# Hybrid GDN/GLA encoder step on one core: two weights' conversions moved ahead of the first copies, sample's transposes widened to 128 rows, the last chunk stored earlier

## The chip, the cores and the metric

The kernel runs on one core of a Trainium2 chip. Its engines are TensorE (PE, matrix products and transposes), VectorE (DVE), ScalarE (ACT), GpSimd (POOL) and SyncE (SP); each works through its own list of instructions in order, and they meet through semaphores. DMA transfers are issued from the lists of SP, POOL and, here and there, ACT. The metric is the device time of one launch in microseconds, smaller is better; of the kernel before there are three timed runs and one profiled execution.

## The reference

One step of a one-layer encoder trunk, for 512 prompt tokens and, with states and caches of their own, 64 sample tokens, at model width 1024, all in float32:

```python
x = x + mixer(rmsnorm(x))        # gated DeltaNet and gated linear attention, merged by gates
x = x + cross_attn(rmsnorm(x))   # 4 heads into 256 memory tokens
x = x + conv_ffn(rmsnorm(x))     # up-projection, depthwise conv, silu gate, down-projection
y = rmsnorm(x) * norm_final
```

In the gated DeltaNet part, tokens go in chunks, and each chunk needs a triangular solve:

```python
kb = kc * bc[..., None]
a_kk = jnp.where(strict, jnp.einsum('nbhcd,nbhsd->nbhcs', kb, kc) * decay, 0.0)
wu = lax.linalg.triangular_solve(eye + a_kk, rhs, left_side=True, lower=True, unit_diagonal=True)
```

The cross attention is `softmax(q k^T / 16) v` per head. The outputs are `y` for prompt and sample, the new states and convolution rows, and the memory's keys and values.

## The kernel before

Features lie on the 128 partitions and the T = 576 tokens (512 prompt, then 64 sample) along the free axis. For a product, a 1024-wide weight comes as tiles of 128 x 1024. To keep float32's accuracy, weight and activation are each split into a high part (`h`, rounded to the format that PE multiplies fast) and a low part (`lo`), and PE forms three products: h by h, h by lo, lo by h (`mm3`).

A weight gets its two parts in `emit_weight` (L621) and `split_summed` (L653): SP loads the raw tile; ACT writes its rounded negative into `lo` (an ACTIVATE with scale −1, "w<-wr") and its rounded copy into `h` (a CAST); then POOL's queue issues a DMA that adds the raw weight from memory to `lo` ("w<-wt", the accumulate), which leaves the rounding error there. A product with that weight's `lo` thus waits for ACT, POOL's queue and the transfer in turn. There are 6 tiles for weight parts (`WB`) and 4 for raw weights (`RAWB = 4`, L29); `weight()` (L717) gives back the parts of weights that are used up, and `fetch` starts later ones.

Nearly all instructions go through a planner, the class `Driver` (L251). It keeps an estimate of when each engine and operand is free, and places an instruction in its engine's list by its planned start; generators of work (`yield`) are run side by side, and products of the large matrices are put between the steps of small chains. So the order on an engine can change where the code that makes a chain changes.

*Start*, in `main` (L1711): the first three weights are split by hand (`wpart`). Then PE multiplies them with all of x, 3 x 8 blocks. `conv_raw` (L1766) makes ACT and DVE copy the three results to `u`; it calls for the results' last product. Only behind it stand `fetch(3)`, which emits the fourth weight and later ones, and the last four calls of `sq_act`. The fourth weight feeds the products ("za") that follow. The small power of the first norm is taken on POOL (`rt`); from it come `dg`, which PE needs to spread the norm over partitions (`rbc`), and `ba`, the input of the gates.

*Sample's triangular solve*, in `c_gdn` (L1135), whose call for sample has n = 64 rows: `xi` holds the inverse as it grows, four heads beside each other. For each of the five `LEVELS`, its odd block columns are copied to `xo`, PE transposes them (L1263), a product with the odd columns of N (`no`, made by `odd_keys`, L1243) follows (L1271), and ACT and DVE mask the result and write it back. `xo` and `no` are tiles of their own; the operands of PE span 64 partitions.

*Sample's attention*, in `c_att` (L1546): `e` holds the exponentials of a group of tokens; the group of the sample has 64 rows. Once per head, two blocks of it are transposed into `pS` (L1591) and copied to `pst`.

*Tail*, from L2344: `half` forms the down-projection's last products, `half_evac` adds them to x, squares and scales; `sums` lets PE add up the squares for a chunk of tokens; `roots` takes the power on DVE and POOL (`rt`); `flip` transposes a chunk (8 transposes) to token-major; `put_out` scales it on ACT and DVE and issues two stores, from SP's list but for one store each of chunks 0 and 1, which ACT issues. Chunks 0 to 3 are prompt's, of 128 tokens; chunk 4 is the sample's 64. In the order of the code: `half(1)` on the first 256 tokens, its evacuation, chunk 3, the sums of chunks 0 and 1, chunk 4, then chunks 0 and 1.

Memory for work tiles is a pool of 57 slots (`NS`) of 584 columns (`SLOT`).

Of the kernel before, what the change touches and what calls it, by code (L numbers as in the profile page):

```python
# [25 lines left out]
SLOT = 584  # L26
HT = T // 2
NS = 57
# [484 lines left out]
def tile_trunk(ctx, tc, xT, memT, wt, wd, vec, cst, w0, wgate, st_gdn, st_conv, st_gla, st_ffn, ckT, cv,  # L513
# [345 lines left out]
    def sum_tile(w=T):  # L859
        acc = slot("acc")  # L860
        G.memset(acc[:, w:w + 8], 0.0)
        return acc
# [10 lines left out]
    def c_rstat(key, accs, n, sample, delay, out=None, at=TP):  # L873
# [8 lines left out]
        if sample:  # L882
            k += 1
            ssq(accs, n, 72, ps)
            G.memset(rin, 1.0)
            V.tensor_scalar(rin[0:64, n:n + 1], ps[0:64, n:n + 1], 1.0 / D, EPS, op0=ALU.mult, op1=ALU.add)
# [196 lines left out]
    def head_norms(*tiles):  # L1083
# [12 lines left out]
        for (o3, n, k), ss in zip(tiles, sums):  # L1096
            on3 = r4(slot("on")[0:n, 0:128 * k])
            V.tensor_tensor(on3, o3, ss[0:n, 0:k].unsqueeze(2).broadcast_to([n, k, 128]), op=ALU.mult)
            ons.append(on3)
# [9 lines left out]
    def head_norm(o3, n, k, box, rq=None):  # L1109
# [13 lines left out]
        on = slot("on")  # L1123
        on3 = r4(on[0:n, 0:128 * k])
# [10 lines left out]
    def c_gdn(h):  # L1135
# [93 lines left out]
        xi = slot("xi")  # L1229
        for i in range(4):  # L1230
            V.scalar_tensor_tensor(xi[0:n, n * i:n * i + n], pk[0:n, n * i:n * i + n], rr[0:n, 4 * SX + i:4 * SX + i + 1],
                                   negm1[0:n, 0:n], op0=ALU.mult, op1=ALU.mult)
# [10 lines left out]
        def odd_keys(li):  # L1243
            no = small(f"no{me}", 2, 256)
            A.copy(no[0:n, 0:w].rearrange("p (a b) -> p a b", b=LEVELS[li]), odd(N_.rearrange("p a b -> p (a b)"), LEVELS[li]))
            return no

        no = odd_keys(0)
        xo = small(f"xo{me}", 1, 256)
# [10 lines left out]
        for li, b in enumerate(LEVELS):  # L1260
            pt = sm()
            for c in range(w // 128):
                PE.transpose(pt[:, n * c:n * c + n], xo[0:n, 128 * c:128 * c + 128], ident[0:n, 0:n])  # L1263
# [6 lines left out]
            for c in range(w // 128):  # L1270
                PE.matmul(p1[:, 128 * c:128 * c + 128], no[0:n, 128 * c:128 * c + 128], even(xi[0:n, 256 * c:256 * c + 256], b), start=True, stop=True)  # L1271
# [3 lines left out]
            if b < LEVELS[-1]:  # L1275
                no = odd_keys(li + 1)
                xo = small(f"xo{me}", 1, 256)
# [22 lines left out]
        if n == 128:  # L1300
            pt2 = sm()
            tt = slot("T2")
            G.memset(tt[0:64, 0:256], 0.0)
            for i in range(4):
                PE.matmul(pt2[64:128, 64 * i:64 * i + 64], N_[:, i, 64:128], xi3[:, i, 0:64], start=True, stop=True)
            V.tensor_copy(tt[64:128, 0:256], pt2[64:128, 0:256])
# [41 lines left out]
        for i in range(4 if h < 4 else 0):  # L1348
            ci = 4 * i + h
            if S is not None:  # L1350
                pc = sm()
                PE.matmul(pc[0:n, 0:128], ks_[i], S, start=True, stop=True)
                R = small("R", 4)[0:n, :]
# [41 lines left out]
    def c_gla(p):  # L1395
# [38 lines left out]
        G.memset(kg[:, T:T + 8], 0.0)  # L1434
# [7 lines left out]
        PE.transpose(pt2[0:72, 0:128], kg[:, TP:T + 8], ident)  # L1442
# [103 lines left out]
    def c_att(hd):  # L1546
# [4 lines left out]
        for g in range(3):  # L1551
# [16 lines left out]
            e = slot("e")  # L1568
            for i in range(cnt_):
# [20 lines left out]
        for mt_ in range(2):  # L1590
            PE.transpose(pS[:, 64 * mt_:64 * mt_ + 64], probs[2][0:64, 128 * mt_:128 * mt_ + 128], ident[0:64, 0:64])  # L1591
        pst = small("pst", 2)
        A.copy(pst, pS[:, 0:128])
# [117 lines left out]
    def main():  # L1711
# [50 lines left out]
        for k in range(KT):  # L1762
            for i, ps in enumerate(first3):
                n, b = divmod(3 * k + i, 8)
                mm3([(ps[:, 0, 0:256], slice(0, 256)), (ps[:, 1, 0:320], slice(256, T))], *ws[n], *xs[k], b, k == 0, k == KT - 1)
        raw_u = [conv_raw(ps, copy) for ps, copy in zip(first3, (V.tensor_copy, V.tensor_copy, A.copy))]  # L1766
        fetch(3)
        for k in range(4, KT):
            sq_act(k)
# [597 lines left out]
        def sums(t):  # L2367
            a, n = toks[t]
            for i, src in enumerate([acc, sqs[t < 2][1]]):
                PE.matmul(pss[0:n, t:t + 1], src[:, a:a + n], ones[:, 0:1], start=i == 0, stop=i == 1)  # L2370
# [29 lines left out]
        for t in (2, 3, 4):  # L2400
            sums(t)
# [3 lines left out]
        put_out(2)  # L2405
        ps = sm()
        yield from half(1, ps[:, 0:256], slice(0, 256))
        half_evac(1, ps, *early)
        flip(3)
        put_out(3)  # L2410
        for t in (0, 1):
            sums(t)
        roots(slice(0, 2), [(128, slice(0, 2))])
        flip(4)
        put_out(4)
# [191 lines left out]
```

## Time and profile before

| | |
|---|---|
| timed runs, median (lowest, highest) | 1081.94 us (1079.63, 1083.07) |
| profiled execution, its own time | 1078.61 us |
| its span in the trace | 1076.8 us |
| mean granted TensorE clock | 0.997 |
| PE busy | 1065.5 us (99%) |
| DVE, ACT, POOL busy | 751.3, 706.9, 363.4 us |
| DMA, mean over the span | 159 GB/s |

A row of a timeline has the start in us, the duration in us, the engine, the line, the operation, the result's tile "<-" the operands' tiles, and a count where neighbours were put together; brackets give the idle time ahead of it and what ended that. All instructions have line L292, that of the helper which records them, so one goes by tiles: `sm` is a PSUM tile, `w` a weight part, `wr` a raw weight, `xh` and `xl` the parts of the normed x, `ach` and `acl` those of other activations, `keep` the identity matrix, `yo` the scaled output, `o_y` the output in memory. A row of windows has, for a stretch of the span, its length, each engine's busy time and count, the granted clock (PEclk, 1.00 is full) and the share of DMA engines at work with GB/s.

### The profile page before, as it was taken

To read this page: it belongs to the slowest core of one execution; us is meant where nothing else is said; L and a number is where in the kernel's file an instruction comes from. 1 tells how busy PE (TensorE), PEld (TensorE's weight loads), DVE (VectorE), ACT (ScalarE), POOL (GpSimd) and SP (SyncE) were. 2 spreads that over 40 slices of the span, in tenths; PEclk is the share of its full clock that TensorE was granted. 3 is DMA by queue.
4 is the path that set the end of the run, shared out by engine and by line. 5 is a ranking of instruction groups with operands and counts; after the bars stand their busy time and mean duration, and the time that the engine had idled before them with its cause. 6 is when DMAs were issued, how large, how long until landed. Compare 5 with 4: busy or idle time off the path is not lost.

```text
span 1076.8 us, 21403 instructions
## 1 busy us (share of the span) xinstructions
PE 1065.5 (99%) x8162; PEld 1048.5 (97%) x8162; DVE 751.3 (70%) x1472; ACT 706.9 (66%) x1410; POOL 363.4 (34%) x584
## 2 busy tenths in 40 slices
PE   9899999999999999999999999999999999999997
PEld 8899999999999999999999999999999999999997
DVE  6666854767665776878647766778877776678665
ACT  6665546564667577456666678768776775777645
POOL 0334225344434333114211235344343333332324
PEclk9999999999999999999999999999999999999999
DMA  7656354454437979679674368758887798778844
GB/s 270 158 124 154 61 135 110 95 123 106 99 58 167 252 171 199 237 208 238 172 186 138 63 161 198 180 115 166 185 192 173 153 217 189 181 159 190 185 87 109
DMA packets 68182, 171.33 MB, mean 159 GB/s; under 512 B 7920, under 2 KB 14576, under 8 KB 68080
## 3 DMA queue, kind: packets, MB, share of 16 engines
q0 software_dynamic: 30672, 71.19, 38.4%
q1 hardware_dynamic: 36976, 98.26, 27.6%
q8 instruction: 64, 1.05, 0.4%
q10 hardware_dynamic: 432, 0.53, 0.1%
q14 instruction: 38, 0.31, 0.1%
HBM read 157.50 MB, written 5.37 MB: 151 GB/s over the span
## 4 chain that ended last, share of the span: by engine, by line
PE 95%; DMA 2%; ACT 1%; DVE 1%; issue 0%; POOL 0%; ACTq 0%; DVEq 0%; POOLq 0%
PE sm L292 95%; DMA w<-wt 2%; ACT w L292 1%; PE warm L292 0%; DVE on L292 0%; ACT jk L292 0%; DVE ws L292 0%; DVE x L292 0%; DVE gt L292 0%; DVE acl L292 0%; DVE yo L292 0%; ACT ao L292 0%; DVE S L292 0%; ACT ach L292 0%; ACT xh L292 0%
## 5 line engine op out<-in xcount | busy, mean ns | idle before, releaser
L292 PE MATMUL sm<-xh,w 128*128 128x290 f32 (+3 forms) x2304 | 448.6, 301 | 3.7 <-DMA w<-wt 3.2
L292 PEld LDWEIGHTS sm<-xh,w 128*128 128x128 f32 x2304 | 358.8, 190 | 6.2 <-DMA w<-wt 3.7
L292 PE MATMUL sm<-xl,w 128*128 128x290 f32 (+3 forms) x1152 | 270.6, 296 | 0.0
L292 POOL DMA_DIRECT2D w<-wt x152 | 135.1, 898 | 348.3 <-ACT w L292 296.5
L292 PE MATMUL sm<-ach,w 128*128 128x288 f32 (+2 forms) x1212 | 231.4, 296 | 0.2 <-DVE x L292 0.2
L292 PEld LDWEIGHTS sm<-xl,w 128*128 128x128 f32 x1152 | 200.7, 189 | 0.2 <-DVE xl L292 0.2
L292 PEld LDWEIGHTS sm<-ach,w 128*128 128x128 f32 x1212 | 189.8, 188 | 1.2 <-ACT w L292 0.6
L292 ACT CAST w<-wr 128x512 fp32r<-128x512 f32 (+5 forms) x209 | 159.2, 764 | 15.2 <-PE sm L292 9.6
L292 ACT ACTIVATE w<-wr 128x512 fp32r<-128x512 f32 (+5 forms) x186 | 142.2, 765 | 27.0 <-PE sm L292 25.8
L292 PE MATMUL sm<-acl,w 128*128 128x256 f32 (+2 forms) x606 | 146.6, 295 | 0.2 <-DVE acl L292 0.2
L292 ACT CAST w<-ws 128x512 fp32r<-128x512 f32 (+1 forms) x136 | 80.2, 597 | 49.9 <-DVE ws L292 26.9
L292 PEld LDWEIGHTS sm<-acl,w 128*128 128x128 f32 x606 | 107.3, 188 | 0.5 <-DVE acl L292 0.5
L292 DVE TENSOR_TENSOR w<-ws,w 128x512 fp32r<-128x512 f32 (+1 forms) x107 | 72.8, 689 | 22.6 <-ACT w L292 20.8
L292 DVE SCALAR_TENSOR_TENSOR fc<-fu,vec,fc 128x578 f32<-128x578 f32 x88 | 70.5, 816 | 3.3 <-ACT fc L292 3.3
L292 PE MATMUL sm<-sh,w 128*128 128x290 f32 x288 | 61.5, 298 | 0.0
L292 DVE TENSOR_TENSOR x<-x,sm 128x320 f32<-128x320 f32 (+3 forms) x98 | 40.1, 438 | 22.8 <-PE sm L292 22.5
L292 POOL DMA_DIRECT2D w<-wd x34 | 29.8, 886 | 75.1 <-ACT w L292 67.6
L292 ACT ACTIVATE fc<-fu,vec 128x578 f32<-128x578 f32 x44 | 38.1, 871 | 15.1 <-POOL fu L292 14.8
L292 PEld LDWEIGHTS sm<-sh,w 128*128 128x128 f32 x288 | 47.6, 189 | 0.0
L292 PE MATMUL sm<-oh,w 128*128 128x256 f32 (+1 forms) x256 | 44.8, 295 | 0.0
L292 DVE TENSOR_TENSOR ws<-ws,wr 128x512 f32<-128x512 f32 (+1 forms) x66 | 43.8, 663 | 1.0
L292 PE MATMUL sm<-sl,w 128*128 128x290 f32 x144 | 39.7, 297 | 0.0
(391 smaller groups left out, 1947.9 us busy)
## 6 DMA issues: line engine op xcount, KB each, us to landing
wr<-wt SPq DMA_DIRECT2D x129, 512.0 KB, 5.6
w<-wt POOLq DMA_DIRECT2D x51, 512.0 KB, 6.7
w<-wt POOLq DMA_DIRECT2D x101, 256.0 KB, 6.1
w<-ws POOLq DMA_DIRECT2D x27, 256.0 KB, 5.1
x<-xT SPq DMA_DIRECT2D x16, 288.0 KB, 5.9
wr<-wt SPq DMA_DIRECT2D x14, 256.0 KB, 5.2
wr<-wd SPq DMA_DIRECT2D x8, 448.0 KB, 5.0
w<-wd POOLq DMA_DIRECT2D x8, 448.0 KB, 6.7
```

The source lines that it names most:

```text
L292: fn(*args, **kw)
```

## The change

- At the start, the last four `sq_act` stand ahead of `conv_raw`, the first three weights are given back, and weights 3 and 4 are emitted there, ahead of `conv_raw`; `fetch(3)` stays behind it.
- In `c_gdn` for the sample, `xo` and `no` lie inside the tile of `xi` (columns 256 to 511), whose lower 64 rows POOL sets to zero; transposes and products take all 128 rows. In `c_att`, POOL zeroes the lower rows of the sample's `e`, the transposes take 128 rows, and the copy picks 64 columns of each 128.
- The head norms write in place, the tile `T2` is laid into that of N, `R` has 2 buffers for 4; pads of 8 columns are 6, `SLOT` is 582, and `NS` is 59.
- In the tail, chunk 4 is transposed and stored ahead of `half(1)` on the first 256 tokens; `sums` is in two parts, and the first part for chunks 0 and 1 stands ahead of chunk 3's output.

```diff
@@ -23,9 +23,9 @@
 NJ = 22
-SLOT = 584
+SLOT = 582
 HT = T // 2
-NS = 57
+NS = 59
 RAWB = 4
@@ -858,7 +858,7 @@
         acc = slot("acc")
-        G.memset(acc[:, w:w + 8], 0.0)
+        G.memset(acc[:, w:w + 6], 0.0)
         return acc
@@ -881,7 +881,7 @@
             k += 1
-            ssq(accs, n, 72, ps)
+            ssq(accs, n, 70, ps)
             G.memset(rin, 1.0)
@@ -1094,7 +1094,7 @@
         for (o3, n, k), ss in zip(tiles, sums):
-            on3 = r4(slot("on")[0:n, 0:128 * k])
+            on3 = o3
             V.tensor_tensor(on3, o3, ss[0:n, 0:k].unsqueeze(2).broadcast_to([n, k, 128]), op=ALU.mult)
@@ -1120,8 +1120,7 @@
         yield
-        on = slot("on")
-        on3 = r4(on[0:n, 0:128 * k])
+        on3 = o3
         V.tensor_tensor(on3, o3, ss[0:n, 0:k].unsqueeze(2).broadcast_to([n, k, 128]), op=ALU.mult)
@@ -1227,6 +1226,9 @@
         xi = slot("xi")
+        rows = P if n == 64 else n
+        if n == 64:
+            G.memset(xi[64:128, 0:512], 0.0)
         for i in range(4):
@@ -1241,12 +1243,12 @@
         def odd_keys(li):
-            no = small(f"no{me}", 2, 256)
+            no = small(f"no{me}", 2, 256) if n == 128 else xi[:, 384:512]
             A.copy(no[0:n, 0:w].rearrange("p (a b) -> p a b", b=LEVELS[li]), odd(N_.rearrange("p a b -> p (a b)"), LEVELS[li]))
...
         no = odd_keys(0)
-        xo = small(f"xo{me}", 1, 256)
+        xo = small(f"xo{me}", 1, 256) if n == 128 else xi[:, 256:384]
         A.copy(xo[0:n, 0:w].rearrange("p (a b) -> p a b", b=2), odd(xi[0:n, 0:W], 2))
@@ -1260,7 +1262,7 @@
             for c in range(w // 128):
-                PE.transpose(pt[:, n * c:n * c + n], xo[0:n, 128 * c:128 * c + 128], ident[0:n, 0:n])
+                PE.transpose(pt[:, 128 * c:128 * c + 128], xo[0:rows, 128 * c:128 * c + 128], ident)
             yc = small(f"yc{me}", 1, 256)
@@ -1268,13 +1270,13 @@
             for c in range(w // 128):
-                PE.matmul(p1[:, 128 * c:128 * c + 128], no[0:n, 128 * c:128 * c + 128], even(xi[0:n, 256 * c:256 * c + 256], b), start=True, stop=True)
+                PE.matmul(p1[:, 128 * c:128 * c + 128], no[0:rows, 128 * c:128 * c + 128], even(xi[0:rows, 256 * c:256 * c + 256], b), start=True, stop=True)
             bd = small(f"bd{me}", 1, 256)
...
                 no = odd_keys(li + 1)
-                xo = small(f"xo{me}", 1, 256)
+                xo = small(f"xo{me}", 1, 256) if n == 128 else xi[:, 256:384]
                 xo_ = xo[0:n, 0:w].rearrange("p (a s b) -> p a s b", s=2, b=b)
@@ -1299,10 +1301,10 @@
             pt2 = sm()
-            tt = slot("T2")
-            G.memset(tt[0:64, 0:256], 0.0)
             for i in range(4):
                 PE.matmul(pt2[64:128, 64 * i:64 * i + 64], N_[:, i, 64:128], xi3[:, i, 0:64], start=True, stop=True)
+            tt = N_[:, 0:2, :].rearrange("p a b -> p (a b)")
+            G.memset(tt[0:64, 0:256], 0.0)
             V.tensor_copy(tt[64:128, 0:256], pt2[64:128, 0:256])
@@ -1350,7 +1352,7 @@
                 PE.matmul(pc[0:n, 0:128], ks_[i], S, start=True, stop=True)
-                R = small("R", 4)[0:n, :]
+                R = small("R", 2)[0:n, :]
                 V.scalar_tensor_tensor(R, pc[0:n, 0:128], sg[0:n, NE, ci:ci + 1], vb[:, i, :], op0=ALU.mult, op1=ALU.add)
@@ -1431,7 +1433,7 @@
         kx, kg = slot("kx"), slot("kg")
-        G.memset(kg[:, T:T + 8], 0.0)
+        G.memset(kg[:, T:T + 6], 0.0)
         V.tensor_tensor(kg[:, 0:T], ks[:, 0:T], e3[:, 0:T], op=ALU.mult)
@@ -1439,7 +1441,7 @@
         pt2 = sm()
-        PE.transpose(pt2[0:72, 0:128], kg[:, TP:T + 8], ident)
+        PE.transpose(pt2[0:70, 0:128], kg[:, TP:T + 6], ident)
         for a in range(2):
@@ -1566,6 +1568,8 @@
             e = slot("e")
+            if g == 2:
+                G.memset(e[64:128, 0:256], 0.0)
             for i in range(cnt_):
@@ -1588,9 +1592,9 @@
         for mt_ in range(2):
-            PE.transpose(pS[:, 64 * mt_:64 * mt_ + 64], probs[2][0:64, 128 * mt_:128 * mt_ + 128], ident[0:64, 0:64])
+            PE.transpose(pS[:, 128 * mt_:128 * mt_ + 128], probs[2][:, 128 * mt_:128 * mt_ + 128], ident)
         pst = small("pst", 2)
-        A.copy(pst, pS[:, 0:128])
+        A.copy(r4(pst, 64), r4(pS[:, 0:256])[:, :, 0:64])
         yield
@@ -1763,10 +1767,14 @@
                 mm3([(ps[:, 0, 0:256], slice(0, 256)), (ps[:, 1, 0:320], slice(256, T))], *ws[n], *xs[k], b, k == 0, k == KT - 1)
+        for k in range(4, KT):
+            sq_act(k)
+        for i in range(3):
+            drop(*wready.pop(i))
+        emit_weight(3)
+        emit_weight(4)
         raw_u = [conv_raw(ps, copy) for ps, copy in zip(first3, (V.tensor_copy, V.tensor_copy, A.copy))]
         fetch(3)
-        for k in range(4, KT):
-            sq_act(k)
         drv.spawn(c_rstat("n1", [(acc, 0)], 4, True, 0.0))
@@ -2364,10 +2372,10 @@
 
-        def sums(t):
+        def sums(t, part):
             a, n = toks[t]
-            for i, src in enumerate([acc, sqs[t < 2][1]]):
-                PE.matmul(pss[0:n, t:t + 1], src[:, a:a + n], ones[:, 0:1], start=i == 0, stop=i == 1)
+            src = sqs[t < 2][1] if part else acc
+            PE.matmul(pss[0:n, t:t + 1], src[:, a:a + n], ones[:, 0:1], start=t == 2 and not part, stop=part, skip_group_check=True)
 
@@ -2398,21 +2406,24 @@
         for t in (2, 3, 4):
-            sums(t)
+            for part in (False, True):
+                sums(t, part)
         roots(slice(2, 5), [(128, slice(2, 4)), (64, slice(4, 5))])
...
         put_out(2)
+        flip(4)
+        put_out(4)
         ps = sm()
...
         flip(3)
+        for t in (0, 1):
+            sums(t, False)
         put_out(3)
         for t in (0, 1):
-            sums(t)
+            sums(t, True)
         roots(slice(0, 2), [(128, slice(0, 2))])
-        flip(4)
-        put_out(4)
         for t in (0, 1):
```

How the planner's lists move, at three places. Names end in a running number, which differs between the two kernels.

On ACT at the start of the program: `sq` is a square of x, `w` the two parts of weights 3 and 4 and `u` the copies of the first results. Before:

```order
L292 ACTIVATE sq_317<-x_89 128x576
L292 COPY u_313<-sm_135 128x256
L292 COPY u_313<-sm_136 128x256
L292 COPY u_313<-sm_136 128x64
L292 ACTIVATE w_357<-wr_355 128x1024
L292 CAST w_356<-wr_355 128x1024
L292 ACTIVATE w_360<-wr_358 128x1024
L292 CAST w_359<-wr_358 128x1024
```

and now:

```order
L292 ACTIVATE sq_314<-x_89 128x576
L292 ACTIVATE w_317<-wr_315 128x1024
L292 CAST w_316<-wr_315 128x1024
L292 ACTIVATE w_320<-wr_318 128x1024
L292 CAST w_319<-wr_318 128x1024
L292 COPY u_323<-sm_135 128x256
L292 COPY u_323<-sm_136 128x256
L292 COPY u_323<-sm_136 128x64
```

The four conversions have changed places with the three copies, which wait for PE's first products.

On PE, one level of sample's triangular solve, between products of large matrices (`ach`, `acl` and `xh` with `w`). Before:

```order
L292 MATMUL sm_4245<-xh_120,w_4075 128x288
L292 MATMUL sm_4245<-xh_124,w_4075 128x288
L292 MATMUL sm_4263<-keep,xo_4202 128x64
L292 MATMUL sm_4267<-xi_3894,no_4201 128x128
L292 MATMUL sm_4274<-ach_3164,w_4109 128x288
L292 MATMUL sm_4274<-acl_3165,w_4109 128x288
```

and now a level of it:

```order
L292 MATMUL sm_4219<-ach_3167,w_4087 128x288
L292 MATMUL sm_4219<-acl_3168,w_4087 128x288
L292 MATMUL sm_4223<-keep,xi_3837 128x128
L292 MATMUL sm_4227<-xi_3837 128x128
L292 MATMUL sm_4219<-ach_3327,w_4087 128x288
L292 MATMUL sm_4219<-acl_3328,w_4087 128x288
```

The two small steps have their operands in one tile and the transpose gives 128 columns; large products still stand on both sides, though not the same ones.

On SP, the stores of `y` at the end of its list, two for a chunk. Before:

```order
L292 DMA o_y<-yo_13587 128x512
L292 DMA o_y<-yo_13588 128x512
L292 DMA o_y<-yo_13616 128x512
L292 DMA o_y<-yo_13617 128x512
L292 DMA o_y<-yo_13636 64x512
L292 DMA o_y<-yo_13637 64x512
L292 DMA o_y<-yo_13652 128x512
L292 DMA o_y<-yo_13666 128x512
```

and now:

```order
L292 DMA o_y<-yo_13567 128x512
L292 DMA o_y<-yo_13568 128x512
L292 DMA o_y<-yo_13582 64x512
L292 DMA o_y<-yo_13583 64x512
L292 DMA o_y<-yo_13611 128x512
L292 DMA o_y<-yo_13612 128x512
L292 DMA o_y<-yo_13630 128x512
L292 DMA o_y<-yo_13645 128x512
```

Chunk 4's two stores (64x512) moved from behind chunk 3's to ahead of them.

## Prediction, before the changed kernel was run

> **What bounds the kernel.** The page of the profile first: its busy times and its chain by engine.
>
> ```profile
> PE 1065.5 (99%) x8162; PEld 1048.5 (97%) x8162; DVE 751.3 (70%) x1472; ACT 706.9 (66%) x1410; POOL 363.4 (34%) x584
> ...
> PE 95%; DMA 2%; ACT 1%; DVE 1%; issue 0%; POOL 0%; ACTq 0%; DVEq 0%; POOLq 0%
> ```
>
> TensorE (PE) is busy for 1065.5 of 1076.8 us and carries 95% of the chain that ends last. The change leaves the number of matmuls as it is. So it can win in three ways only: less idle time of PE, PE time that was run slower than it need be, and what follows PE's last product. The view of waits says what ended PE's idle time (total, number, longest, in us):
>
> ```profile
> PE sm L292 <- DMA w<-wt: 3.2, 2, 2.8
> PE warm L292 <- POOL acc L292: 1.0, 1, 1.0
> PE sm L292 <- ACT gt L292: 0.4, 1, 0.4
> ```
>
> One wait is 2.8 us long and is for a weight; all others are at most 1.0 us. PE's timeline places it:
>
> ```profile
> 35.90 0.80 PE L292 MATMUL sm<-xh,w 128*128 128x256 f32 x4 [2.84 <-DMA w<-wt]
> 36.54 0.77 PE L292 MATMUL sm<-dg,onesr 128*128 128x512 f32 x4
> 37.15 3.18 PE L292 MATMUL sm<-xh,w 128*128 128x256 f32 x12
> 40.12 1.41 PE L292 MATMUL sm<-cst,ba 128*128 128x8 f32 x10
> ```
>
> PE stands still from 33.06 (35.90 − 2.84) to 35.90. The table of windows around it, cut where the granted clock changes:
>
> ```profile
> core 0: us, PE busy (x) PEld busy (x) DVE busy (x) ACT busy (x) POOL busy (x), PEclk, DMA share, GB/s
> ...
> 33.79:37.20 3.41, 1.30 (x9) 1.21 (x9) 0.00 (x0) 0.00 (x0) 0.00 (x0) 1.00 1.05 274
> 37.20:40.62 3.42, 3.42 (x17) 3.42 (x16) 2.30 (x6) 1.23 (x4) 1.10 (x4) 0.50 1.05 277
> 40.62:44.03 3.41, 3.41 (x19) 2.41 (x20) 2.12 (x8) 2.79 (x6) 0.22 (x1) 1.00 0.40 89
> ```
>
> The window with the wait is followed by one of equal length at clock 0.50, in which PE is busy throughout, and then by full clock.
>
> **The change, part by part.** All terms are against the profiled execution (1078.61 us, of which 1076.84 is the span). It lies 3.3 us below the median of the timed runs, 1081.94; I subtract the same sum from that median.
>
> *Start: the wait.* The late weight is the fourth. Where it comes from, on ACT, on POOL, in the chain of waits, and for the tile w around it:
>
> ```profile
> 15.62 4.12 ACT L292 ACTIVATE sq<-x 128x576 f32<-128x576 f32 x7
> 25.43 0.77 ACT L292 COPY u<-sm 128x256 f32<-128x256 f32 x3 [5.69 <-PE sm L292]
> 26.07 1.08 ACT L292 ACTIVATE w<-wr 128x1024 fp32r<-128x1024 f32 x1
> ```
>
> ```profile
> 27.46 1.05 POOL L292 DMA_DIRECT2D w<-wt  x1 [24.57 <-ACT w L292]
> ```
>
> ```profile
> 27.46 8.39 DMA w<-wt
> ```
>
> ```profile
> DMA to landing us min/median/max: 5.5/8.9/12.0
> ```
>
> ```profile
> 23.40:25.40 2.00, 2.00 (x17) 1.90 (x15) 1.54 (x6) 0.00 (x0) 0.00 (x0) 1.00 0.00 0
> ```
>
> ACT squares until 19.74 (15.62 + 4.12), then idles 5.69 us for the copies of `u`, which need PE's first three products, and only then makes the negated half at 26.07. POOL's accumulate follows at 27.46 and lands 8.39 us later, when PE resumes. The change puts two weights' conversions ahead of the copies: ACT starts the first at 19.74. From ACT's start to POOL's issue is 27.46 − 26.07 = 1.39, so the issue is at about 21.2. Its tiles were the first weight's, which only the first third of those products reads. At 8.39 us it lands at 29.5, at the longest landing in the row, 12.0, at 33.2, against a need at 33.06. The DMA engines moved nothing from 23.40 to 25.40, so the transfer has room. The 2.84 us go; bounds 2.7 (longest landing) and 2.84.
>
> What is late next? PE's next operand is `dg`, then `ba`:
>
> ```profile
> 32.08 1.12 DVE L292 TENSOR_SCALAR dg<-keep,rl 128x64 fp32r<-128x64 f32 x1
> ...
> 37.82 0.82 DVE L292 TENSOR_TENSOR ba<-sm,rbc 128x256 f32<-128x256 f32 x2 [4.62 <-ACT rbc L292]
> ```
>
> ```profile
> 37.20 0.70 ACT L292 COPY rbc<-sm 128x512 f32<-128x512 f32 x2 [5.34 <-PE sm L292]
> ```
>
> `dg` is ready at 33.20 and PE now comes to it at 33.06 + 0.64 (35.90 to 36.54) = 33.70: no wait. Its products end 0.61 later (36.54 to 37.15), at 34.31. From there `ba` took 38.64 − 37.15 = 1.49, so it is ready at 35.80; PE needs the twelve products' 2.97 us (37.15 to 40.12) at twice the clock, 1.49, and comes at 35.80 too. That is a tie. I price it at 0.1, bounds 0 and 0.3. **Start: 2.7.** The copies of `u` now stand behind two more pairs of conversions (2.1 us a pair: 26.07 to 28.1), which end at about 23.9, before ACT's copy could start at 25.43: nothing lost. POOL's third accumulate stands ahead of the small power op for `dg`, but its conversion stays behind the copies, so it issues near 27.5, when POOL issued one before: nothing either.
>
> *Start: the half clock.* At 0.50 the window did 3.42/2 = 1.71 us of work. If the wait caused it, **1.7** goes; bounds 0 and 1.71. I take 1.7, because the half clock follows the wait at once and full clock is back one window later. [...]
>
> *Sample's transposes in c_gdn: five levels.* A level on 64 rows:
>
> ```profile
> 319.41 0.29 PE L292 MATMUL sm<-acl,w 128*128 128x288 f32 x1
> 319.63 0.27 PE L292 MATMUL sm<-keep,xo 64*128 64x64 f32 x1
> 319.75 0.44 PE L292 MATMUL sm<-xi,no 64*128 64x128 f32 x2
> 320.11 0.40 PE L292 MATMUL sm<-ach,w 128*128 128x288 f32 x1
> ```
>
> and one on 128 rows, for prompt tokens, with twice the work:
>
> ```profile
> 87.65 0.38 PE L292 MATMUL sm<-keep,xo 128*128 128x128 f32 x2
> 87.87 0.62 PE L292 MATMUL sm<-xi,no 128*128 128x128 f32 x4
> 88.24 0.53 PE L292 MATMUL sm<-xh,w 128*128 128x256 f32 x2
> ```
>
> From the product at 319.41 to the next at 320.11 is 0.70, less the product's own 0.13 (288 columns at the pace of 256 in 0.118): 0.57. On 128 rows it is 0.11 (0.22/2) + 0.19 (0.37/2) = 0.30. So 0.27 a level, five levels: **1.4**; bounds 0, if the loss comes back elsewhere, and 1.6.
>
> *Sample's transposes in c_att: four heads.*
>
> ```profile
> 557.27 0.54 PE L292 MATMUL sm<-keep,e 128*128 128x128 f32 x3
> 557.74 0.53 PE L292 MATMUL sm<-xh,w 128*128 128x256 f32 x2
> ```
>
> This group is one transpose of 128 rows and two of 64: 0.47 us, against 3 × 0.11 = 0.33 at the pace above. 0.14 × 4 = **0.6**; bounds 0 and 0.9. The added memsets of POOL (one for `xi`, four for `e`) have no row in this trace; POOL is busy 34%, so 0 on the path unless late (a rival below). [...]
>
> *The rest of the middle.* Head norms in place, a tile fewer, 59 slots for 57 and the shorter pads leave PE's work alone; two buffers of `R` for four and `no` in one place can add waits. PE's order changes in the middle with products still between the small steps. I take **−0.2**, bounds −1 and +0.4 (the 0.4 us wait above).
>
> *Tail.*
>
> ```profile
> 1068.06 2.79 PE L292 MATMUL sm<-keep,gx 128*64 128x128 f32 x24
> ```
>
> ```profile
> 1068.48 0.70 POOL L292 TENSOR_TENSOR rtf<-rin,mhalf 128x2 f32<-128x2 f32 x1 [3.04 <-DVE rin L292]
> ```
>
> ```profile
> 1070.09 1.55 DVE L292 TENSOR_SCALAR yo<-sm,rtf 128x512 f32<-128x512 f32 x2 [0.20 <-PE sm L292]
> ```
>
> ```profile
> DMA to landing us min/median/max: 2.0/2.6/3.9
> ```
>
> ```profile
> 1071.00:1072.00 1.00, 0.00 (x0) 0.00 (x0) 0.64 (x1) 0.14 (x1) 0.00 (x0) 1.00 0.95 170
> ...
> 1073.00:1074.00 1.00, 0.00 (x0) 0.00 (x0) 0.00 (x0) 0.00 (x0) 0.00 (x0) 1.00 1.05 399
> ```
>
> The 24 transposes are those of chunks 4, 0 and 1. Chunk 4's eight (0.9 us) move ahead of `half(1)`, so PE's last still ends at 1070.85. The root of chunks 0 and 1 then comes 0.9 later (1069.2 to 1070.1), beside the first flips in place of chunk 4's: ACT's first copy moves by some 0.4, DVE's last, which starts behind PE's last flip, does not and ends at 1071.64. The gain is in the queue: chunk 4's two stores go out in front, under PE's products, on SP's queue past both stores of chunk 3, which start later by up to 0.9. The slow stretch (170 GB/s in the microsecond from 1071) is where 64-row stores lie among the others; behind them 399. The last stores should land in about 3.1 rather than 3.9: **0.8**, bounds 0 and 3.9 − 2.3 = 1.6 (2.3 between least and median).
>
> Sum: 2.7 + 1.7 + 1.4 + 0.6 − 0.2 + 0.8 = **7.0**. Against the profile: 1071.6; against the median: **1074.9**.
>
> **Rivals.** *The wait only moves* (0.13). The accumulate now runs beside the loads of raw weights, or `ba` is late. The landing row's 12.0 speaks for it, the empty 23.40:25.40 against. A new wait of 2 us that leaves the clock alone gives 1076.9, one of 1 us that brings the half clock (1.7) gives 1077.6: about 1077.3.
>
> *The half clock stays* (0.08), because it is not the wait that brings it: 7.0 − 1.7 = 5.3, so 1076.6.
>
> *Narrow transposes are the cheaper ones* (0.03): if one of 64 rows took half of 0.11, widening 13 of them (five `xo`, eight `e`) would cost 13 × 0.055 = 0.7 and the 2.0 saved would not come: 7.0 − 2.7 = 4.3, so 1077.6. The 0.12 us between 319.63 and 319.75, for one of 64 rows, says no. [...]
>
> *The middle gives it back, so the change does not do what it says* (0.11). Shared buffers and another order put waits of some 0.7 us at sample's five levels and four heads: 9 × 0.7 = 6.3, so 1081.2. For it: `xi`, `xo` and `no` in one tile. Against it: PE's longest wait in the whole middle is 0.4.
>
> *Slower: a memset behind a queue* (0.05).
>
> ```profile
> POOL w L292 <- ACT w L292: 428.1, 142, 24.6
> ...
> 551.89 0.86 POOL L292 DMA_DIRECT2D w<-wt  x1 [9.74 <-ACT w L292]
> ```
>
> POOL's accumulates wait for ACT, 3.0 us in the mean (428.1/142). The zeros of `xi` and `e` stand in that queue. In the new order the first head's memset follows this accumulate, done at 552.75, and the transposes come at 557.47: 4.7 us to spare. It decides once a memset ends later than that. Then PE waits 3.0 and loses a half-clock window's 1.7: 4.7 at each of five memsets, 23.5 less the gain of 7.0: 16.5 slower, 1098.4.
>
> **How the numbers follow.** Forecast 0.60, rivals 0.13, 0.08, 0.03, 0.11, 0.05. The bounds of the terms give 2.4 (2.7 − 0.3) + 0 + 0 + 0 − 1 + 0 = 1.4 at one end and 2.84 + 1.71 + 1.6 + 0.9 + 0.4 + 1.6 = 9.0 at the other: 1080.5 and 1072.9. That all terms fall to their low ends together is unlikely, and the timed runs themselves lie up to 2.3 us from their median, so I take 1079.5 and 1071.0: this holds the forecast and all rivals but the last two. A measurement of this kernel can tell about 0.3% (3.2 us) from no change, so below 1078.7 is faster: the forecast but for a twelfth (0.55), two thirds of the first rival (0.09) and the next two (0.10), 0.74 and, with a share of the fourth, 0.76. Within 0.3%: the rest of the forecast and of the first, most of the fourth, 0.18. Slower 0.06.
>
> **What would show it.** The wait of 2.84 at 35.90 gone, and clock 1.00 in 37.20:40.62; if one goes without the other, the clock term is wrong. Rows `xo` and `e` of 128 rows with steps of 0.11 and ordinary products right behind; no wait of PE over 0.5 us between 160 and 640 us. In the tail, the last copy within 0.2 us of its place behind PE's last product, and landings near 3.1. The forecast is wrong if PE's busy time does not fall by some 3.7 us (1.7 + 1.4 + 0.6).

## The result, and the profile after

The changed kernel takes 1068.99 us (median of five, 1068.92 to 1069.65), the kernel before in the same comparison 1081.94 (five, 1079.16 to 1083.63): ratio 0.989, 95% interval 0.987 to 0.991. The forecast was 1074.9 with a range of 1071.0 to 1079.5. The direction was right, the gain was forecast at 7.0 us and came out at 12.95, and the time lies below the range. From profiled execution to profiled execution it is 1078.61 − 1068.99 = 9.6.

The page of the changed kernel, its busy times and its chain by engine:

```profile
PE 1059.6 (99%) x8162; PEld 1045.0 (98%) x8162; DVE 749.7 (70%) x1480; ACT 704.6 (66%) x1410; POOL 356.5 (33%) x581
...
PE 96%; DMA 1%; ACT 1%; issue 0%; DVE 0%; SPq 0%; ACTq 0%
```

PE still bounds it, with as many instructions and 5.9 us less busy time. Its waits (total, number, longest):

```profile
PE warm L292 <- POOL acc L292: 1.0, 1, 1.0
PE sm L292 <- ACT gt L292: 0.4, 1, 0.4
...
PE sm L292 <- DMA w<-wt: 0.2, 1, 0.2
```

The wait of 2.8 us is gone, and nothing has taken its place. How the fourth weight now gets ready, on ACT, on POOL, and in the view of tile w from 20 to 36 us:

```profile
19.69 1.05 ACT L292 ACTIVATE w<-wr 128x1024 fp32r<-128x1024 f32 x1
```

```profile
21.05 1.05 POOL L292 DMA_DIRECT2D w<-wt  x1 [18.19 <-ACT w L292]
```

```profile
DMA to landing us min/median/max: 7.6/10.0/10.9
```

Conversion at 19.69 (forecast 19.74), accumulate at 21.05 (21.2). Even the longest of the three landings would end at 31.95, before PE's first product with it at 32.62. PE's timeline and the windows at that place:

```profile
32.35 0.43 PE L292 MATMUL sm<-xl,w 128*128 128x256 f32 x2
32.62 0.69 PE L292 MATMUL sm<-xh,w 128*128 128x256 f32 x4
33.15 0.77 PE L292 MATMUL sm<-dg,onesr 128*128 128x512 f32 x4
33.75 1.84 PE L292 MATMUL sm<-xh,w 128*128 128x256 f32 x12
35.44 1.16 PE L292 MATMUL sm<-cst,ba 128*128 128x8 f32 x10
```

```profile
33.79:37.20 3.41, 3.41 (x26) 3.13 (x26) 2.74 (x9) 2.41 (x6) 1.26 (x6) 1.00 0.55 143
37.20:40.62 3.42, 3.42 (x22) 2.70 (x21) 3.00 (x9) 2.59 (x6) 0.93 (x1) 1.00 0.01 2
```

PE is busy throughout at full clock, and it reaches `ba` at 35.44 for 40.12: 4.7 us earlier. One level of sample's solve, one group of the attention's transposes, and the view of the output tile:

```profile
321.92 0.30 PE L292 MATMUL sm<-acl,w 128*128 128x288 f32 x1
322.05 0.27 PE L292 MATMUL sm<-keep,xi 128*128 128x128 f32 x1
322.16 0.39 PE L292 MATMUL sm<-xi 128*128 128x128 f32 x2
322.30 0.38 PE L292 MATMUL sm<-ach,w 128*128 128x288 f32 x1
```

```profile
550.93 1.25 PE L292 MATMUL sm<-keep,e 128*128 128x128 f32 x10
551.94 1.83 PE L292 MATMUL sm<-xh,w 128*128 128x256 f32 x12
```

```profile
DMA to landing us min/median/max: 2.0/2.4/3.2
```

A level is 322.30 − 322.05 = 0.25 us, where it was 0.57 on 64 rows; ten transposes of `e` run at 0.10 each into the next product, with no gap. The longest store takes 3.2 us, where it took 3.9.

The first products of `ba` with `wg`, in the kernel before and in the changed one:

```profile
41.46 2.38 PE L292 MATMUL sm<-ba,wg 128*128 128x512 f32 x8
```

```profile
36.53 2.38 PE L292 MATMUL sm<-ba,wg 128*128 128x512 f32 x8
```

So the difference by stage, from starts of the same product in both traces, is 4.9 us here, 8.2 by the first product of tile `sh` (its rows stand below), 9.1 by its last, and 9.6 at the end.

### The profile page after: what moved, and what is told of

It reads as the page before. It is cut to its first block, busy times and chain, and to the rows that moved or that the text cites. A ratio compares the mean times of both kernels' runs of the same rounds, so it can differ in the third digit from the quotient of the medians.

```text
span 1067.2 us, 21405 instructions
## 1 busy us (share of the span) xinstructions
PE 1059.6 (99%) x8162; PEld 1045.0 (98%) x8162; DVE 749.7 (70%) x1480; ACT 704.6 (66%) x1410; POOL 356.5 (33%) x581
## 4 chain that ended last, share of the span: by engine, by line
PE 96%; DMA 1%; ACT 1%; issue 0%; DVE 0%; SPq 0%; ACTq 0%
PE sm L292 96%; DMA w<-wt 1%; ACT w L292 1%; DMA wr<-wt 0%; ACT gt L292 0%; DVE w L292 0%; DVE x L292 0%; DVE acl L292 0%; DVE yo L292 0%; ACT ao L292 0%; ACT ach L292 0%; ACT xh L292 0%; DVE xl L292 0%; SPq L292 0%; DVE ws L292 0%
```

## Experiments

Four questions: is the start's gain what the forecast took it for, where do the 3.3 us between the median and the profiled execution of before come from, what did the rows bring, and what the pools, which were priced at nothing?

**The kernel before, again.** No edit.

> The kernel before, unchanged, for its spread and a second trace. Theory V (the wait for the fourth weight is not the same in each execution, and costs more in most than in the profiled one): executions spread over some 4 us again (1079 to 1084), the slower ones at a lower mean clock, and a trace that is slower than 1078.6 shows a longer wait ahead of the fourth weight's products (above 2.84 us) or more than one half-clock window behind it. Rival W (the spread lies elsewhere, in PE's pace or in the DMA of the whole run): the start of a slower trace is that of the first, 4.6 us lost, and the difference is spread over the span.

Twelve executions: nine at 1078.2 to 1080.0, three at 1082.7 to 1082.9 with a mean clock of 0.993; 23 runs of before beside this group have a median of 1078.58, three of them above 1081.8. So the kernel before has a usual time near 1078.6, which its first profiled execution showed, and in about one of six executions it takes 3 to 5 us more. With those beside the later groups, 17 of 95 executions lie between 1081.5 and 1083.6, all others between 1076.6 and 1080.4. Three of the five that made the median of 1081.94 were of the longer kind by their times (1081.94, 1083.07 and 1083.63); no clock is on record for them. That part of theory V holds; its other part, a longer wait, does not (see the last traces).

**The start alone.**

```diff
+        for k in range(4, KT):
+            sq_act(k)
+        for i in range(3):
+            drop(*wready.pop(i))
+        emit_weight(3)
+        emit_weight(4)
```

> Before with the start part alone. Theory V: the spread falls below 1.2 us, and the median falls by 4.9 (the profiled start) plus the 3.3 that lay between the median and the profiled execution: some 8 us, to about 1073.7. Rival W: 4.9 us less than the runs beside it and the spread of 4 us stays. The forecast's own sum for this part was 4.4.

1073.72 (1073.12 to 1074.13), 4.9 less than the 1078.58 beside it, ratio 0.9945 [0.9929, 0.996]; no execution is near 1078. The 1073.7 of theory V was met, but by luck, against another base: 4.9 is the typical loss, and the 4 us of one execution in six go as well.

**All but the start.** The changed kernel with that edit undone.

> The changed kernel with the start part undone. Theory V: the spread of before is back (3 to 5 us), the median is 1069.0 + 8 = 1077, some 4.7 less than before. Rival W: 1069.0 + 4.9 = 1073.9 and a spread of under 1 us, as in the changed kernel.

1074.47 (1073.62 to 1075.64), a wait of 3.3 us and one half-clock window in its trace: 5.5 above the changed kernel. That is near rival W's 1073.9 and misses theory V's 1077, which was reckoned from the median of the first five. The six executions spread over 2.0 us, and none took the 4 us more, which for one in six says little.

**The tail alone.**

```diff
         put_out(2)
+        flip(4)
+        put_out(4)
         ps = sm()
         yield from half(1, ps[:, 0:256], slice(0, 256))
```

> Before with the tail part alone. The forecast's sum: 0.8 us less (bounds 0 and 1.6); the two traces differ in the tail by 0.6. By theory V the median hardly tells (spread of 4 us); the trace does: from the last product's start to the end of the span 0.5 to 0.8 less than before's 6.1 + 0.2.

1078.62 against 1078.58, ratio 0.9999 [0.9986, 1.0011]: not to be told in the median. In the trace the longest landing of a store is 3.3 us for 3.9, and from the last product of tile `sh`, of the feed-forward part, to the end of the span it is 65.4 us (1011.4 to 1076.8) for 65.9 (1010.9 to 1076.8): 0.5 less, at the low end of the 0.5 to 0.8 expected.

**The wait filled.** What the clock costs, apart from the time of the wait.

```diff
+            if not filled:
+                filled.append(sm())
+                for _ in range(13):
+                    drv.put(drv.now, [(nc.tensor.matmul, (filled[0], ones_r, ones_r.unsqueeze(1).broadcast_to([P, 4, 128])), dict(start=True, stop=True))])
             for k in range(n):
```

> Before, with 13 products of ones into a spare PSUM tile (2.8 us) placed where PE stands still for the fourth weight's low part; their result is not used. It parts the wait from the clock: the wait's time stays lost, but PE is busy in it. Theory V (the wait brings the half clock, for none, one or more windows by chance): no half clock after 6.5 us, so 1.7 less than the typical execution of before (1078.6), 1076.9, spread under 1.5 us and none near 1082.5; mean clock 0.998 or more in every run. Rival (the half clock at 37 us comes from elsewhere, or from the short gaps): half clock stays, 1078.6, and some runs near 1082.5.

1076.91 (1076.02 to 1077.47) against 1079.15 beside it, ratio 0.9975 [0.9965, 0.9985], none of twelve above 1077.5, where 6 of 35 beside it were above 1081.5. PE's timeline of this run:

```profile
32.95 3.13 PE L292 MATMUL sm<-onesr 128*128 128x512 f32 x13
35.92 0.80 PE L292 MATMUL sm<-xh,w 128*128 128x256 f32 x4
...
37.17 1.85 PE L292 MATMUL sm<-xh,w 128*128 128x256 f32 x12
...
39.95 2.38 PE L292 MATMUL sm<-ba,wg 128*128 128x512 f32 x8
```

The low part's products start at 35.92, as before (35.90), but the twelve products behind them take 1.85 us for 3.18, and those with `wg` start at 39.95 for 41.46. Same delay but PE busy in it, and no half clock: in this kernel it is PE's idle time that brings it, and its price is 1.5 us up to there (41.46 − 39.95). The median holds more than that, 2.2 us: the spare tile also moves the order of the middle, where the wait of 0.4 us for `gt` is gone, and the place of later tiles, and the products of `sh` take 286.6 us (722.2 to 1008.8) for 287.5.

**A longer wait.**

```diff
         A.copy(h, raw)
+        if not held:
+            held.append(slot("sq"))
+            G.tensor_tensor(held[0][:, 0:512], f(lo)[:, 0:512], f(lo)[:, 512:1024], op=ALU.add)
         drv.accumulate(lo, src, nc.gpsimd)
```

> Before, with a sum of 512 columns on POOL (result unused) between the fourth weight's conversion and its accumulate, which also puts that accumulate behind the norm's power: the issue moves from 27.5 to about 29.9 and the wait from 2.8 to about 5.2. Theory V: a longer wait more often fills a whole window of the clock's gate, so more runs show 2 or 3 half-clock windows (mean clock 0.993 to 0.995): median 1078.6 + 2.4 + 1.7 to 3.9 = 1082.7 to 1084.9. Rival (clock loss independent of the wait's length): 1081.0 with the same share of slow runs as before (8 in 47).

A miss: 1080.12 (1079.49 to 1080.79), the wait 4.67 us, all ten executions between 0.995 and 0.997, none at 0.993. It is below both theory V's 1082.7 and the rival's 1081.0; neither had counted on the feed-forward part, which ran 0.9 us faster here (rows below, at the slots of 582 columns). Windows of its trace (columns as before the change: length, busy times, PEclk, DMA share, GB/s):

```profile
33.03:36.44 3.41, 0.00 (x0) 0.00 (x0) 0.00 (x0) 0.00 (x0) 1.09 (x8) 1.00 1.04 233
36.44:39.85 3.41, 2.45 (x9) 2.26 (x10) 0.00 (x0) 0.23 (x1) 0.00 (x0) 0.50 1.08 267
39.85:43.26 3.41, 3.41 (x17) 3.41 (x16) 2.30 (x6) 1.07 (x5) 1.10 (x4) 0.50 0.83 162
43.26:46.68 3.42, 3.42 (x19) 2.42 (x19) 2.13 (x8) 2.72 (x6) 0.26 (x1) 1.00 0.01 2
```

An empty window, then one with 0.96 us idle at half clock, a full one at half clock, and full clock again: two windows. A longer wait does not by itself bring the four.

**The rows alone.**

```diff
-                PE.transpose(pt[:, n * c:n * c + n], xo[0:n, 128 * c:128 * c + 128], ident[0:n, 0:n])
+                PE.transpose(pt[:, 128 * c:128 * c + 128], xo[0:rows, 128 * c:128 * c + 128], ident)
...
-            PE.transpose(pS[:, 64 * mt_:64 * mt_ + 64], probs[2][0:64, 128 * mt_:128 * mt_ + 128], ident[0:64, 0:64])
+            PE.transpose(pS[:, 128 * mt_:128 * mt_ + 128], probs[2][:, 128 * mt_:128 * mt_ + 128], ident)
```

> Before with the 128-row transposes of c_gdn and c_att alone, no pool, pad or buffer changes. The forecast's sum: 1.4 + 0.6 = 2.0 less. The changed kernel's trace gained 1.7 between 165 and 540 us and 1.0 between 540 and 640: if the rows alone do that, 2.5 to 2.8 less, 1075.9. Rival (part of it comes from the other order that pools and pads bring): 1.5 to 2.0 less, and the steps in the trace give the rest.

1077.81 against 1079.15, ratio 0.9984 [0.9972, 0.9996]: less than the forecast's 2.0. Six of the 35 executions beside it are of the longer kind; against the median of the other 29, 1078.65, it is 0.8. Its waits show why:

```profile
PE sm L292 <- ACT gt L292: 1.0, 1, 1.0
PE warm L292 <- POOL acc L292: 1.0, 1, 1.0
PE sm L292 <- POOL ol L292: 0.5, 1, 0.5
PE sm L292 <- ACT oh L292: 0.4, 1, 0.4
```

With shorter steps the planner starts the output projection earlier (first product of `oh` at 342.8 for 347.3), ahead of the head norms that feed it. Waits for `oh` and `ol` (0.5, 0.4 and 0.3) and 0.6 more for `gt` are 1.8 us, most of what the rows save: added up from start to start between 47 us and the first product of `sh`, the steps with a small product take 192.0 us for 194.6 before, so the rows save 2.6.

**Slots of 582 columns.** `SLOT = 582` and the pads, nothing else.

> Before with slots of 582 columns for 584 and the pads that go with it (6 for 8), still 57 slots. The changed kernel gained 1.3 us between 640 and 1060 us, where both issue the same products in the same order, 0.5 ns a product in the mean. Theory P (pitch: where the moving operands begin in memory): the products of 290 columns take 134.9 ns in the mean for 135.5, and this kernel gains about 1.3 there, 1077.3. Rival Q (which slots hold what, by 59 for 57): 135.5 as before, and no gain, 1078.6.

1077.96 against 1079.15, ratio 0.9985 [0.9972, 0.9998]; against the 29 usual executions beside it, 0.7 less. But the edit does not change the pitch: in the programs as they are built, slots lie 2336 bytes apart on a partition in this kernel, in the kernel before and in the changed one (582 columns of 4 bytes would be 2328). Theory P is thus not tested by it, and pitch is no part of the changed kernel's gain. What the feed-forward part's pace depends on, the 288 products of tile `sh` tell, which are the same in the same order in all kernels here. First and last start, in the kernel before, here, with the longer wait (57 slots of 584), and in the changed kernel:

```profile
L292 PE MATMUL sm<-sh,w x288: 290/297/316, 723.4 to 1010.9; 128*128 128x290 f32 x144
```

```profile
L292 PE MATMUL sm<-sh,w x288: 290/297/402, 722.2 to 1009.4; 128*128 128x290 f32 x144
```

```profile
L292 PE MATMUL sm<-sh,w x288: 292/298/377, 726.0 to 1012.6; 128*128 128x290 f32 x144
```

```profile
L292 PE MATMUL sm<-sh,w x288: 289/297/306, 715.2 to 1001.8; 128*128 128x290 f32 x144
```

The stretch is 287.5 us before, 287.2 here, and 286.6 both with the longer wait and in the changed kernel. In the six traces with slots as in the kernel before (its own four, the start alone, the tail alone) it is 287.5 or 287.6, in the ten others 286.4 to 287.2. The trace of the kernel before that comes to it 4.9 us later (the last one below) has 287.5 too, so a later start is not what shortens it.

The kernel with the longer wait has, but for a few rows on POOL at the start, the order of before on every engine; it only takes one slot more at the start, so that later tiles lie elsewhere. In the built programs, 1212 of the 2142 products from the first of `sh` to the last have their activation at another address than before, and none its weight or its result; with the start alone 36 have, with the tail alone none. So neither another pitch nor more slots is needed, and rival Q falls as it was put. That it is the place of the activations' tiles is what is left for that kernel; which tiles, and in what way, no run here shows. The 0.3 of this run says little: the rows alone and the next kernel, which differ in 34 of these addresses, have 287.0 and 286.7.

**Three parts together**: start, rows and tail, without pools, pads, in-place norms and buffer counts.

> Start, 128-row transposes and tail together on before, without the slots, pads, in-place norms and buffer counts. If those make no difference of their own, this is the changed kernel but for where tiles lie: 1069.0 to 1069.6, no run near 1073. If they carry part of the gain (shorter waits in the middle, more room), 1070 to 1071. The single parts in the traces add up to 4.9 (start) + 2.0 to 2.5 (rows, with its later effects) + 0.6 (tail) = 7.5 to 8.0, which would be 1070.6 to 1071.1.

1071.32 (1070.90 to 1071.88), 7.7 less than the 1078.99 beside it, ratio 0.9915 [0.9894, 0.9936], and 2.3 above the changed kernel: the single parts add up to it nearly (1071.1). PE near 360 us:

```profile
355.12 0.54 PE L292 MATMUL sm<-oh,w 128*128 128x256 f32 x2 [0.35 <-ACT oh L292]
355.92 0.53 PE L292 MATMUL sm<-ol,w 128*128 128x256 f32 x2 [0.26 <-DVE ol L292]
...
357.87 0.54 PE L292 MATMUL sm<-ol,w 128*128 128x256 f32 x2 [0.49 <-POOL ol L292]
```

The same waits as with the rows alone, 1.8 us with the longer one for `gt`. The changed kernel has none of them, so something in what was priced at nothing keeps them away.

**Which of it?** First all but the in-place norms and T2, then the in-place norms without the pool, pads, T2 and `R`. The edit of the norms:

```diff
-            on3 = r4(slot("on")[0:n, 0:128 * k])
+            on3 = o3
```

> The changed kernel without the in-place head norms and without the tile T2 laid into N: with 59 slots, shorter pads and two buffers of R. The start, rows and tail alone gave 1071.3, with 1.1 us of waits near 360 us for the head norms' outputs (oh, ol) that the changed kernel's trace does not have; the changed kernel gives 1069.0. Theory R (room: more slots let chains start earlier): 1069.0 to 1069.5 and no wait for oh or ol. Rival I (the norms in place are what shortens it): 1071.3 and those waits.

> Start, rows, tail and the head norms in place, with 57 slots of 584 columns, T2 a tile of its own and four buffers of R. Theory R: 1071.3 and waits of PE for oh or ol near 360 us. Rival I: 1069.0 to 1069.5 and none. If both this and the run ahead of it lie between 1069.5 and 1071, or neither reaches 1069.5, it takes both.

1072.65 (ratio 0.9939 [0.9918, 0.9959]) and 1071.48 (0.9928 [0.9906, 0.995]): neither reaches 1069.5. Both show the waits, as in this row of the first's waits:

```profile
PE sm L292 <- POOL ol L292: 0.5, 1, 0.5
```

By the expectation it takes both. But the tile T2 laid into N is missing from both kernels, so that this alone, or only together with the rest, keeps the waits away is not ruled out. Which of the second's missing pieces (slots, T2, `R`) it needs was not parted.

The first's trace (1073.62) shows more: its waits of 0.35, 0.26 and 0.49 us fall into one window, and half clock follows here too.

```profile
354.34:357.75 3.41, 2.31 (x13) 1.58 (x12) 3.25 (x7) 3.22 (x6) 1.72 (x2) 1.00 0.90 194
357.75:361.16 3.41, 3.41 (x15) 3.41 (x16) 3.02 (x6) 2.18 (x4) 1.49 (x2) 0.50 0.64 132
```

In the traces of the second, of the three parts and of the rows alone, with the same waits, full clock stays: from 345 to 540 us it is 1.00 in the last two, and the second has a mean of 0.999 over its span.

**The wait half filled**: as the filled wait, with 5 products for 13.

> As the filled wait, but with 5 products of ones (1.1 us) in place of 13, so that some 1.8 us of PE's 2.8 to 3.2 idle remain. In the traces the granted clock changes on a grid of 3.41 us, and a window with 1.86 us idle or more was followed by half clock, one with 1.30 or less was not. Theory G (half clock follows where more than about half of one window is idle): now many runs see at most 0.9 to 1.8 idle in each of two windows and keep full clock; a share of about half at 0.998 or more, median between 1076.9 and 1078.6, no run near 1082.5. Rival (any long gap brings it): all at 0.997, 1078.6, and some near 1082.5.

1077.73 (1076.29 to 1078.69) against 1078.99, none of twelve above 1078.7. Only two of twelve have a mean clock of 0.999 (1076.29 and 1076.60), where eight of twelve have 0.999 or more with the wait filled: in the trace 2.08 us of idle remained, not 1.8, and lay in one window:

```profile
32.98:36.39 3.41, 1.33 (x7) 0.81 (x7) 0.00 (x0) 0.00 (x0) 0.16 (x3) 1.00 1.03 265
36.39:39.80 3.41, 3.41 (x15) 3.22 (x14) 1.33 (x3) 0.70 (x2) 0.00 (x0) 0.50 1.05 274
```

It had 1.33 us of work, and half clock followed. Theory G's direction holds, its share does not. Nor does idle time alone decide: half clock followed on 1.10 us idle in the trace at 357 us above, and did not follow on 1.28 us idle in the second trace of the kernel before, where the wait's first part fell into the window ahead:

```profile
31.04:34.46 3.42, 2.14 (x17) 1.90 (x15) 2.29 (x4) 0.94 (x2) 2.50 (x11) 1.00 1.04 253
34.46:37.87 3.41, 1.50 (x10) 1.41 (x11) 0.00 (x0) 0.20 (x1) 0.00 (x0) 1.00 1.05 275
```

**Two more traces of the kernel before.**

> The kernel before, for a trace: about one execution in six takes 4 us more at a mean clock of 0.993, which is 3 to 4 half-clock windows. If this is one, theory S (the gap ends inside a window that already runs at half clock, and the small products of the gates count as little work in the next) expects half clock from about 34 to 46 us, and nothing else changed; rival: a second stretch of half clock elsewhere. If it is a usual one: one window, 1078 to 1080.

> One more trace of the kernel before, with the same two readings as in the run ahead of it: theory S if it is a slow one (half clock from about 34 to 46 us), else one half-clock window and 1078 to 1080.

The first was a usual one (1078.53). The second took 1083.46, and its windows show what the 4 us more are:

```profile
32.14:35.55 3.41, 0.59 (x5) 0.35 (x3) 0.73 (x1) 0.00 (x0) 0.94 (x6) 1.00 1.05 253
35.55:38.96 3.41, 2.95 (x11) 2.76 (x12) 0.12 (x1) 0.70 (x2) 0.00 (x0) 0.50 1.07 278
38.96:42.37 3.41, 3.41 (x17) 3.41 (x16) 2.18 (x6) 1.10 (x3) 1.10 (x4) 0.50 0.81 196
42.37:45.79 3.42, 3.42 (x10) 2.34 (x11) 1.14 (x6) 2.32 (x5) 0.19 (x1) 0.50 0.01 4
45.79:49.20 3.41, 3.41 (x11) 2.38 (x11) 2.94 (x7) 1.62 (x2) 0.68 (x1) 0.50 0.61 84
49.20:52.61 3.41, 3.41 (x28) 3.41 (x27) 3.31 (x6) 3.32 (x5) 0.00 (x0) 1.00 0.79 223
```

Four half-clock windows, 35.55 to 49.20, and nowhere else while PE works: 3 × 1.71 = 5.1 us more than one window, of which 4.9 are there at the first product of `sh` (728.2, for 723.3 in the usual trace ahead of it). The wait itself is 3.28 us, for 3.25 in the usual one. Only the grid lies otherwise: the window behind the drop still has 0.46 us idle, and the next ones hold the gates' products with 8 columns (from 41.29) and those with `wg`. The run with slots of 582 columns has nearly the same grid (its window behind the drop begins at 35.49) but a wait of 2.95 us, and 0.20 us idle there; it has one half-clock window. That fits theory S; that these products count as little work was not tested by itself. Why none of the twenty executions of that run and of the rows alone took the 4 us more, with waits of 3.0 and 3.1 us in their traces and the start's lists of before, stays open.

## Why the prediction was right and wrong, step by step

**Start, the wait: right.** The conversions, the issue and the landing came where the working put them, and nothing was late next; `ba`, the tie, cost nothing. With the clock the forecast had 4.4, measured were 4.9: PE came to `dg` 0.55 us earlier than the working had it (33.15, not 33.70). Half of that is a small error of size. Rows of products overlap (the group at 32.35 lasts 0.43, the next starts 0.27 behind it), so that the low part's products would have started some 0.16 before 33.06, and they take 0.53 without the wait, not the 0.64 behind it. The other half lies ahead of it and is most likely the place of the clock's grid, not the change: full clock began at 5.0 us in this execution and at 6.5 in that of before, and PE's first product with `xh` started at 5.49 for 5.86.

**Start, the half clock: right, and shown.** Filling the wait left the delay and took the half clock away, 1.5 us by the products with `wg` for the 1.7 forecast. It did not take a window without any work: windows with 1.30 us of work (the kernel before), 1.33 (the wait half filled) and 2.31 (all but the in-place norms) were followed by half clock, as was the empty one of the longer wait. What measure of work decides stays open, since one with 2.14 us (the second trace of the kernel before) was not.

**c_gdn and c_att: right in the step, wrong in what follows it.** A level fell from 0.57 to 0.25, five levels 1.6 for the forecast's 1.4, and all the steps together 2.6 for 2.0. But the rows alone shifted the planner's order into new waits of 1.8 us: for that kernel the rival "the middle gives it back" is what happened, by waits for the head norms' outputs and not at the levels and heads where the rival had them.

**The rest of the middle: wrong.** The working said that head norms in place, more slots and fewer buffers "leave PE's work alone" and priced them at −0.2. Without them the rows' waits come: 1071.3 without, 1069.0 with, and the waits are 1.8 of these 2.3 us. Between the start's stage and the first product of `sh` the traces differ by 8.2 − 4.9 = 3.3 us, where the forecast had 1.4 + 0.6 − 0.2 = 1.8. Of the 3.3, the rows' steps where no wait takes them back are 2.6; the other 0.7 stay open.

**A term that the sum did not have.** The same products of the feed-forward part run 0.9 us faster from 715 to 1002 us (8.2 to 9.1), and by 0.3 to 1.1 us in every kernel here but the start alone and the tail alone, which have the tiles of that part, but for a few, where before has them.

**Tail: right.** 9.6 − 9.1 = 0.5, and 0.8 was forecast; the tail alone has the same 0.5, with the longest landing 3.3 us for 3.9. That it is the 64-row stores lying among the others that slow the queue was not tested apart from their place in it.

**From the profile to the median: the step that failed, and the largest error.** The working set the profiled execution 3.3 us below the median and subtracted "the same sum from that median", as if the 3.3 were an offset that both kernels have. It was not: 1078.61 is the usual time of before (78 of 95 executions lie between 1076.6 and 1080.4), 1081.94 is one of the longer kind, and that kind, with four half-clock windows behind the wait for one in the trace that caught it, leaves with the wait. The changed kernel's median equals its profiled execution. So the miss of 5.9 is 3.3 from the base and 2.6 from the sum (9.6 less 7.0): 0.5 at the start, 1.5 in the middle, 0.9 in the feed-forward part, less 0.3 in the tail. That the longer kind made the median was bad luck as well: at 17 in 95, three or more of five come about four times in a hundred (an estimate). Against a usual execution of before the change is worth about 9.6 us, or 0.9%.

**The slower rival** did not come: PE nowhere waits for the memsets of `e` and `xi`. None of its products with these tiles shows idle time ahead of it, and its longest wait behind the first microsecond is the 0.4 us for `gt`.

## What to carry to other kernels

Price an idle gap of the engine that bounds a kernel by what it does to the clock behind it (here 2.84 us of wait, and 1.71 us for the half-clock window behind it), and ask how often: where runs of a kernel spread by more than its stages explain, look for the gap that only sometimes falls badly. Here, with the start alone, six executions lay between 1073.12 and 1074.13, where 23 of before lay between 1076.64 and 1082.63; and with the whole change the median moved by 12.95 us, where the two profiled executions differ by 9.6. A step that is made shorter in a planned kernel moves what the planner starts next (with the rows alone into 1.8 us of waits, for 2.6 saved); test it together with the buffers that the earlier start needs. And time a part alone before calling its neighbour free, and take the base of a forecast from enough executions to see whether they are of one kind.

## What was not expected of the hardware

In the traces of these runs the granted clock changes on a grid of 3.41 us whose place differs between executions: full clock began between 4.8 and 7.2 us, and the half clock behind the wait lasted 3.42 us in the kernel before (37.20 to 40.62), 6.82 with the longer wait (36.44 to 43.26) and 13.65 in the last trace of before (35.55 to 49.20). One and the same wait of the kernel before was followed by one half-clock window at 3.25 us and by four at 3.28, and three short waits of 1.10 us together in one window were enough once (half clock from 357.75 to 361.16). And the 287.5 us of identical products in identical order were 286.4 to 287.2, 0.3 to 1.1 less, in ten kernels that place their tiles otherwise, without a wait to be seen in the trace; in one of them, 0.9 us faster, only activations lie elsewhere.
